# A hybrid decoder layer in split fp32: products with w's high half first, and Strassen pairs for the mixer's in and out projections

## The chip, the core and the metric

One core of a Trainium2 chip runs the whole layer. Its engines work in parallel, each through its own queue in order: TensorE (PE) multiplies, VectorE (DVE) and ScalarE (ACT) do element-wise work and empty the accumulators in PSUM, GpSimd (POOL) does a few small steps and issues accumulating DMAs, SyncE (SP) issues the loads. The metric is the device time of one execution in microseconds.

## The reference, cut to what matters

Sequence 256, width 2048, one layer; all in float32.

```
x = x + 0.5 * swiglu(rmsnorm(x, g1), w_gate1, w_up1, w_down1)      # w_gate, w_up: 2048 x 5632
h = rmsnorm(x, g_mix)
a_q, a_k, a_v, m_q, m_k, m_v, m_o, m_i, m_f = split(h @ w_in)      # 1024 1024 1024 512 512 1024 1024 4 4
y_a = diff_attention(a_q, a_k, a_v)        # 4 heads, two causal softmaxes each, their difference times a_v
q, k = silu(causal_conv4(m_q, m_k))
y_b = rmsnorm(mlstm(q, k, m_v, m_i, m_f)) * sigmoid(m_o)           # 4 heads, decays from the gates i and f
x = x + concat(y_a, y_b) @ w_out                                   # 2048 x 2048
x = x + 0.5 * swiglu(rmsnorm(x, g2), w_gate2, w_up2, w_down2)
out = rmsnorm(x, g_final)
```

## The kernel before

**Split products.** Every weight and every activation is written as a high half (a rounded fp32r copy, made by ACT) and a low half (the remainder, made by DVE): `split`, lines 112 to 114. A product of two tiles is then three matmuls into one accumulator (`mm3`, 139 to 143): x high by w high (141), x high by w low (142), x low by w high (143). The stationary side is 128 x 128 of x transposed, the moving side 512 columns of w.

**Plain units.** `units` (174) multiplies a chunk of 512 columns of w by x: for each unit of two k tiles (256 rows of w) it loads 512 KB of weights (or takes half of a 1 MB load, `load_w`), splits them (`split_w`), and multiplies them by both token halves (`hb` 0 and 1): 2 x 2 x 3 = 12 matmuls. `linear` (213) runs all units of a chunk: 96 matmuls.

**Strassen pairs.** `Paired` (322) takes two chunks at once, wa and wb. The 2 x 2 blocks (two k tiles by two chunks against two token halves by two k tiles) are multiplied in seven products (Strassen's scheme in Winograd's form) rather than eight: a pair costs 21 matmuls, not 24. `first` (337) loads the pair's four tiles, makes three sums on DVE (350, 352), splits sums and tiles, and issues four of the products into four accumulator banks; `combine` (364) adds the banks up with two ACT copies and four DVE operations; `second` (386) issues the other three products (`bare`, `upper`) and, as plain units, the k tiles that are in no pair, for the first chunk; `third` (417) yields the plain units of the second chunk one by one. x needs sums too: `sum_pair` (265). `NP` = 4 of 8 pairs are made so in the feed-forward projections.

**The chain.** `Chain.run` (444) weaves runs together: while the pairs of a new run are issued, the plain units of the last run's second chunk (`third`) are issued between them; then come the new run's `combine`, the end of the old chunk, and the new run's `second`. Small steps that become ready (transposes of a finished part, say) are put on the list `pending`, and `flush` issues all of them at once: behind the first step of `second`, and in `units` before unit 3.

**The mixer.** Only the two feed-forward parts use pairs. The mixer's chunks are all `linear`: three narrow ones for the mLSTM's q and k (392, 384, 256 columns), two for m_v (761 to 770), two each for a_q and a_k (826 to 829), two for a_v (885), two for m_o (903). Between them stand, each as a block over four heads: convolution and SiLU, the mLSTM's score matrices (773 to 788), its numerators (799 to 810), the attention's scores and softmax (833 to 867), and the weighted sums (886 to 899). The out projection (926 to 930) is four `units` streams.

**What sets the order.** The kernel is written as one program; a scheduler places each engine's instructions by priority. `tc.high_priority(offset=AHEAD)` moves loads, splits and a few chains of small steps forward by 400 places, so that they run ahead of the products that use them; how far is limited by the buffers (4 tiles each for wh and wl, 6 accumulator banks, 21 slots for transposed activations). After that each engine runs strictly in its order and waits on semaphores.

## Time and profile before

| | |
|---|---|
| median of 3 runs | 1826.5 us (1823.06 to 1829.19) |
| the profiled execution | 1824.08 us |
| its span, first to last instruction | 1822.4 us |
| mean granted clock of TensorE | 0.998 of 2.4 GHz |
| PE, DVE, ACT, POOL busy | 98%, 82%, 62%, 9% |
| bytes moved | 397.72 MB, 218 GB/s |
| first feed-forward part, mixer and out projection, second feed-forward part | to about 720 us, to about 1130 us, to the end |

A busy share says how long an engine had an instruction in flight; matmuls overlap, so two kernels with PE at 98% may differ in how many matmuls they run per microsecond. "Idle before" and "waits" count the time in which PE had nothing in flight, and name what ended it.

### The profile page before, as it was taken

What the parts mean: (1) busy time and instruction counts of PE and PEld (TensorE: products, weight loads), DVE (VectorE), ACT (ScalarE), POOL (GpSimd) and SP (SyncE); (2) the same over time, 40 slices, a digit from 0 to 9 for tenths busy, and PEclk for the clock granted to TensorE, in tenths of its full rate; (3) what the DMA queues carried; (4) which work ended last, traced back from release to release, by engine and by line L of the source; (5) the groups of instructions that cost most, each with busy time, mean ns of one, the idle gap of its engine ahead of it and who ended that gap; (6) DMA issues with size and microseconds to landing.
All of it is one profiled execution on the core that took longest, in us unless ns stands there. A gap on an engine that the chain in (4) does not pass through costs nothing.

```text
span 1822.4 us, 22684 instructions
## 1 busy us (share of the span) xinstructions
PE 1794.6 (98%) x8090; PEld 1468.2 (81%) x8090; DVE 1488.8 (82%) x1775; ACT 1121.7 (62%) x1443; POOL 156.3 (9%) x199
## 2 busy tenths in 40 slices
PE   8999999999999999999999999999999999999998
PEld 6788788878887888978888888788787888887886
DVE  6889889988998887674465578899889988998886
ACT  6666666666666666554455456666666666666664
POOL 0001100111002100000000000101110021002100
PEclk9999999999999999999999999999999999999999
DMA  8667877797688874553544565677877798678864
GB/s 333 215 204 235 222 234 232 246 250 220 210 252 247 259 237 146 200 185 121 185 159 164 185 213 179 199 228 241 234 230 225 256 247 243 208 230 256 253 190 155
DMA packets 114449, 397.72 MB, mean 218 GB/s; under 512 B 12960, under 2 KB 12960, under 8 KB 107424
## 3 DMA queue, kind: packets, MB, share of 16 engines
q1 hardware_dynamic: 88560, 349.28, 55.5%
q0 software_dynamic: 24480, 44.58, 14.2%
q10 hardware_dynamic: 1296, 2.42, 0.4%
q8 instruction: 63, 1.03, 0.2%
q14 instruction: 50, 0.41, 0.1%
HBM read 349.56 MB, written 2.10 MB: 193 GB/s over the span
## 4 chain that ended last, share of the span: by engine, by line
PE 76%; DMA 9%; DVE 8%; issue 4%; ACT 2%; SPq 1%; POOL 0%; POOLq 0%; DVEq 0%; ACTq 0%
PE acc L142 24%; PE acc L143 24%; PE acc L141 24%; DMA raw<-in_wu_dram 6%; DVE wl L114 5%; ACT wh L113 2%; DVE sums L350 2%; DMA raw<-raw 1%; PE tr L296 1%; SPq L166 1%; DMA xres<-in_x_dram 1%; DVE raw L352 1%; DMA xraw<-in_xt_dram 1%; DMA raw<-in_wd_dram 0%; PE num L808 0%
## 5 line engine op out<-in xcount | busy, mean ns | idle before, releaser
L113 ACT CAST wh<-raw 128x1024 fp32r<-128x1024 f32 (+3 forms) x503 | 464.3, 931 | 377.2 <-PE acc L143 360.9
L114 DVE TENSOR_TENSOR wl<-raw,wh 128x1024 fp32r<-128x1024 f32 (+3 forms) x503 | 535.1, 1074 | 194.7 <-ACT wh L113 191.1
L142 PE MATMUL acc<-wl,xt 128*128 128x512 f32 (+3 forms) x1632 | 630.4, 386 | 4.2 <-DVE wl L114 4.0
L141 PE MATMUL acc<-wh,xt 128*128 128x512 f32 (+3 forms) x1632 | 630.7, 387 | 2.6 <-ACT xt L108 1.5
L143 PE MATMUL acc<-wh,xt 128*128 128x512 f32 (+3 forms) x1632 | 628.8, 386 | 1.2 <-DVE xt L109 1.2
L114 DVE TENSOR_TENSOR wl<-rawp,wh 128x1024 fp32r<-128x1024 f32 x284 | 346.7, 1222 | 43.8 <-ACT wh L113 37.1
L113 ACT CAST wh<-rawp 128x1024 fp32r<-128x1024 f32 x284 | 298.8, 1053 | 117.1 <-PE acc L143 96.4
L141 PE MATMUL acc<-wh,xs 128*128 128x512 f32 x902 | 355.7, 397 | 8.4 <-ACT wh L113 4.0
L142 PEld LDWEIGHTS acc<-wl,xt 128*128 128x128 f32 x1632 | 306.5, 188 | 67.9 <-DVE wl L114 8.8
L141 PEld LDWEIGHTS acc<-wh,xt 128*128 128x128 f32 x1632 | 306.0, 188 | 65.5 <-ACT wh L113 2.8
L143 PEld LDWEIGHTS acc<-wh,xt 128*128 128x128 f32 x1632 | 306.3, 188 | 62.1 <-DVE xt L109 2.5
L142 PE MATMUL acc<-wl,xs 128*128 128x512 f32 x902 | 352.7, 391 | 1.3 <-DVE wl L114 1.1
L143 PE MATMUL acc<-wh,xs 128*128 128x512 f32 x902 | 350.9, 390 | 0.1
L113 ACT CAST wh<-sums 128x1024 fp32r<-128x1024 f32 x122 | 128.4, 1053 | 144.4 <-PE acc L143 139.2
L141 PEld LDWEIGHTS acc<-wh,xs 128*128 128x128 f32 x902 | 169.1, 188 | 57.2 <-ACT u L371 9.3
L142 PEld LDWEIGHTS acc<-wl,xs 128*128 128x128 f32 x902 | 169.4, 188 | 38.9 <-DVE wl L114 6.4
L143 PEld LDWEIGHTS acc<-wh,xs 128*128 128x128 f32 x902 | 169.3, 188 | 36.0 <-DVE xs L109 1.0
L361 POOL DMA_DIRECT2D raw<-raw x122 | 104.0, 853 | 1030.9 <-DVE wl L114 973.7
L350 DVE TENSOR_TENSOR sums<-raw 128x1024 f32<-128x1024 f32 x122 | 149.2, 1223 | 39.4 <-DMA raw<-in_wu_dram 29.2
L114 DVE TENSOR_TENSOR wl<-sums,wh 128x1024 fp32r<-128x1024 f32 x122 | 149.0, 1222 | 14.7 <-ACT wh L113 14.7
L352 DVE TENSOR_TENSOR raw<-sums,raw 128x512 f32<-128x512 f32 x122 | 83.8, 687 | 0.5
L282 POOL DMA_DIRECT2D xres<-part x48 | 43.6, 1060 | 238.2 <-ACT part L281 238.2
(194 smaller groups left out, 756.0 us busy)
## 6 DMA issues: line engine op xcount, KB each, us to landing
rawp<-in_wd_dram SPq DMA_DIRECT2D x96, 512.0 KB, 5.7
rawp<-in_wu_dram SPq DMA_DIRECT2D x94, 512.0 KB, 7.6
raw<-in_wg_dram SPq DMA_DIRECT2D x89, 512.0 KB, 6.7
rawp<-in_wg_dram SPq DMA_DIRECT2D x86, 512.0 KB, 5.7
raw<-in_wu_dram SPq DMA_DIRECT2D x82, 512.0 KB, 7.5
raw<-in_wd_dram SPq DMA_DIRECT2D x80, 512.0 KB, 6.3
raw<-in_win_dram SPq DMA_DIRECT2D x40, 1024.0 KB, 4.8
raw<-raw POOLq DMA_DIRECT2D x122, 256.0 KB, 6.3
```

The lines of the kernel that those rows point to most:

```text
L113: nc.scalar.copy(hi, src)
L114: nc.vector.tensor_tensor(out=lo, in0=src, in1=hi.bitcast(F32), op=ALU.subtract)
L141: nc.tensor.matmul(acc, lh, rh, start=first, stop=False, skip_group_check=on)
L142: nc.tensor.matmul(acc, lh, rl, start=False, stop=False, skip_group_check=on)
L143: nc.tensor.matmul(acc, ll, rh, start=False, stop=last, skip_group_check=on)
L166: nc.sync.dma_start(dst, w[k // LK][:, k % LK:k % LK + 2, :])
L282: nc.gpsimd.dma_start(xres[:, hb, c * CW:(c + 1) * CW], t, accum_op=ALU.add)
L296: nc.tensor.transpose(tr[:, i, hb * P:(hb + 1) * P], hs[hb][:, k * P:(k + 1) * P], ident)
L350: nc.vector.tensor_tensor(out=sums, in0=raw[:, 0:4:3, :], in1=raw[:, 2:3, :].to_broadcast([P, 2, CW]), op=ALU.add)
L352: nc.vector.tensor_tensor(out=raw[:, 2, :], in0=sums[:, 0, :], in1=raw[:, 3, :], op=ALU.add)
L361: nc.gpsimd.dma_start(raw[:, 2, :], raw[:, 1, :], accum_op=ALU.add)
```

## The change

- `mm3` is replaced by `mms`, which takes a list of products: for each, x high by w high and x low by w high (lines 145 and 146 of the changed kernel), and only then, for each, x high by w low (148). A list is one half of a pair's first products (two products), a `bare` or `upper` step, or a whole plain unit with both token halves.
- In the mixer, a_q, m_v, a_k, a_v and m_o (in this order) are five chained `Paired` runs with `NP_MIX` = 3 pairs of eight; the out projection is two, with `NP_OUT` = 2. The third of the narrow q/k chunks is put into the chain as a stream of plain units with loads of their own.
- The blocks over four heads are cut into steps for one head. `side` holds the convolution and gate steps, `mid` the scores, numerators, attention and weighted sums; `aside` issues one of each per step of a run. `flush(n)` issues the first n entries of `pending`. In the run of the first two out-projection chunks, two entries are issued ahead of the first pair (`lead`).
- `vec` and `act` wrap DVE and ACT so that each small operation gets the priority of `soon()` (440 places ahead). The convolution's first step goes from DVE to ACT and its SiLU is done per head and in place. `xp2` and `yT` get sums for their first pairs. The gate matrices use a transpose bank rather than an accumulator bank.

The core of the diff:

```
-    def mm3(acc, lh, ll, rh, rl, first, last, on=False):
-        nc.tensor.matmul(acc, lh, rh, start=first, stop=False, skip_group_check=on)
-        nc.tensor.matmul(acc, lh, rl, start=False, stop=False, skip_group_check=on)
-        nc.tensor.matmul(acc, ll, rh, start=False, stop=last, skip_group_check=on)
+    def mms(jobs):
+        for acc, lh, ll, rh, rl, first, last, on in jobs:
+            nc.tensor.matmul(acc, lh, rh, start=first, stop=False, skip_group_check=on)
+            nc.tensor.matmul(acc, ll, rh, start=False, stop=False, skip_group_check=on)
+        for acc, lh, ll, rh, rl, first, last, on in jobs:
+            nc.tensor.matmul(acc, lh, rl, start=False, stop=last, skip_group_check=on)
...
-                self.prod(self.p5, j, S1, f, 0, at, end)
-                self.prod(self.p7, j, S3, f, 1, at, end)
-                self.prod(self.p1, j, A1, e, 0, at, end)
-                self.prod(self.p6, j, S2, e, 1, at, end)
+                mms([self.job(self.p5, j, S1, f, 0, at, end), self.job(self.p7, j, S3, f, 1, at, end)])
+                mms([self.job(self.p1, j, A1, e, 0, at, end), self.job(self.p6, j, S2, e, 1, at, end)])
...
+    def flush(n=None):
+        now = pending[:n]
+        del pending[:n]
+        for f in now:
             f()
...
+    class Early:
+        def __init__(self, engine):
+            self.engine = engine
+        def __getattr__(self, op):
+            def run(*args, **kwargs):
+                with soon():
+                    return getattr(self.engine, op)(*args, **kwargs)
+            return run
+    vec, act = Early(nc.vector), Early(nc.scalar)
+    side, mid = [], []
+    def aside(work):
+        if work:
+            work.pop(0)()
...
             for i in range(max(self.ns, len(self.rest))):
+                aside(side)
...
-                if i == 0:
+                if i % 2 == 0:
                     flush()
+                aside(mid)
...
+        def run(self, p, half, end, last_units=1, lead=()):
             done = 0
+            for f in lead:
+                next(self.stream)
+                done += 1
+                f()
             for i, _ in enumerate(p.first()):
                 while done < (i + 1) * self.steps // p.ns:
                     next(self.stream)
                     done += 1
+                flush(1)
+                aside(side)
...
+    def conv(acc, src, h, i):
+        w = lambda j: prm[:, G_CW + j * 8 + i:G_CW + j * 8 + i + 1]
+        a = acc[:, h, :]
+        act.activation(a, src[:, h, :], AF.Identity, scale=w(3), bias=prm[:, G_CB + i:G_CB + i + 1])
+        for d in (1, 2, 3):
+            vec.scalar_tensor_tensor(a[:, d:], src[:, h, :S - d], w(3 - d), a[:, d:], op0=ALU.mult, op1=ALU.add)
+        act.activation(a, a, AF.Silu)
...
+    def both(c):
+        return Paired(xp2, win[c], win[c + 1], KD, NP_MIX)
...
+    chain.run(both(2), to_T(qT), to_T(qT))
+    by_head(scores)
+    chain.run(both(0), functools.partial(take_mv, 0), functools.partial(take_mv, 1))
+    by_head(numerators)
+    chain.run(both(4), to_T(kT), to_T(kT))
+    by_head(attend)
+    chain.run(both(6), take_av, take_av)
+    chain.run(both(8), functools.partial(gate_out, 0), functools.partial(gate_out, 1))
...
-    for c in range(4):
-        accs = []
-        chain.put(units(accs, yT, wout[c], KD, fine=c == 3), KD // UK, functools.partial(finish_out, c, accs))
-        if c < 3:
-            chain.finish()
+    for c in (0, 2):
+        chain.run(Paired(yT, wout[c], wout[c + 1], KD, NP_OUT), functools.partial(finish_out, c),
+                  functools.partial(finish_out, c + 1),
+                  lead=() if c else [functools.partial(flush, 1)] * 2)
```

Two places show what this does to PE's order. The first is a pair's first products in the first feed-forward part; `wh` and `wl` are the weights' halves, `xs` the token sums' halves, and the `acc` tiles four accumulator banks. PE's rows before:

```order
L141 MATMUL acc_417_2067<-wh_419_2071,xs_4_133 128x512 [waits Activation_49]
L142 MATMUL acc_417_2067<-wl_420_2072,xs_4_133 128x512 [waits DVE_49]
L143 MATMUL acc_417_2067<-wh_419_2071,xs_5_134 128x512
L141 MATMUL acc_416_2066<-wh_419_2071,xs_4_133 128x512
L142 MATMUL acc_416_2066<-wl_420_2072,xs_4_133 128x512
L143 MATMUL acc_416_2066<-wh_419_2071,xs_5_134 128x512
L141 MATMUL acc_414_2064<-wh_422_2076,xs_4_133 128x512 [waits Activation_49]
L142 MATMUL acc_414_2064<-wl_423_2077,xs_4_133 128x512 [waits DVE_49]
L143 MATMUL acc_414_2064<-wh_422_2076,xs_5_134 128x512
L141 MATMUL acc_415_2065<-wh_422_2076,xs_4_133 128x512 [waits Activation_49]
L142 MATMUL acc_415_2065<-wl_423_2077,xs_4_133 128x512
L143 MATMUL acc_415_2065<-wh_422_2076,xs_5_134 128x512
```

Each accumulator's three products stand together. In the changed kernel:

```order
L145 MATMUL acc_417_2067<-wh_419_2071,xs_4_133 128x512 [waits Activation_49]
L146 MATMUL acc_417_2067<-wh_419_2071,xs_5_134 128x512
L145 MATMUL acc_416_2066<-wh_419_2071,xs_4_133 128x512
L146 MATMUL acc_416_2066<-wh_419_2071,xs_5_134 128x512
L148 MATMUL acc_417_2067<-wl_420_2072,xs_4_133 128x512 [waits DVE_49]
L148 MATMUL acc_416_2066<-wl_420_2072,xs_4_133 128x512
L145 MATMUL acc_414_2064<-wh_422_2076,xs_4_133 128x512 [waits Activation_49]
L146 MATMUL acc_414_2064<-wh_422_2076,xs_5_134 128x512
L145 MATMUL acc_415_2065<-wh_422_2076,xs_4_133 128x512 [waits Activation_49]
L146 MATMUL acc_415_2065<-wh_422_2076,xs_5_134 128x512
L148 MATMUL acc_414_2064<-wl_423_2077,xs_4_133 128x512 [waits DVE_49]
L148 MATMUL acc_415_2065<-wl_423_2077,xs_4_133 128x512
```

The products with `wl` stood second in each product and now stand behind all four with `wh`; the number of matmuls is the same.

The second is the mLSTM's numerators in the mixer: `num` is an accumulator bank, `mv` the values, `dec` a head's weighted scores. PE's rows before:

```order
L808 MATMUL num_1433_7090<-mv_1393_6878,dec_1420_7040 128x257 [waits PE_49,Activation_49,Pool_49]
L808 MATMUL num_1434_7094<-mv_1393_6878,dec_1420_7040 128x257 [waits DVE_49]
L808 MATMUL num_1434_7094<-mv_1394_6881,dec_1420_7040 128x257 [waits Pool_49]
L808 MATMUL num_1435_7099<-mv_1393_6878,dec_1423_7053 128x257 [waits PE_49,Activation_49]
L808 MATMUL num_1436_7103<-mv_1393_6878,dec_1423_7053 128x257 [waits DVE_49]
L808 MATMUL num_1436_7103<-mv_1394_6881,dec_1423_7053 128x257
L808 MATMUL num_1437_7108<-mv_1417_7029,dec_1426_7066 128x257 [waits PE_49,Activation_49,Pool_49]
L808 MATMUL num_1438_7112<-mv_1417_7029,dec_1426_7066 128x257 [waits DVE_49]
L808 MATMUL num_1438_7112<-mv_1418_7032,dec_1426_7066 128x257 [waits Pool_49]
L808 MATMUL num_1439_7117<-mv_1417_7029,dec_1429_7079 128x257 [waits DVE_49,PE_49]
L808 MATMUL num_1440_7121<-mv_1417_7029,dec_1429_7079 128x257 [waits DVE_49,PE_49]
L808 MATMUL num_1440_7121<-mv_1418_7032,dec_1429_7079 128x257
```

All twelve stand in one row. In the changed kernel, the step of the second head and the products behind it:

```order
L846 MATMUL num_1578_7705<-mv_1518_7430,dec_1489_7274 128x257 [waits DVE_49,PE_49]
L846 MATMUL num_1579_7709<-mv_1518_7430,dec_1489_7274 128x257 [waits DVE_49,PE_49]
L846 MATMUL num_1579_7709<-mv_1519_7433,dec_1489_7274 128x257
L145 MATMUL acc_1520_7436<-wh_1580_7714,xs_1261_6022 128x512 [waits Activation_49]
L146 MATMUL acc_1520_7436<-wh_1580_7714,xs_1262_6023 128x512
L145 MATMUL acc_1522_7438<-wh_1580_7714,xs_1261_6022 128x512
L146 MATMUL acc_1522_7438<-wh_1580_7714,xs_1262_6023 128x512
L148 MATMUL acc_1520_7436<-wl_1581_7715,xs_1261_6022 128x512
L148 MATMUL acc_1522_7438<-wl_1581_7715,xs_1261_6022 128x512
L145 MATMUL acc_1523_7439<-wh_1582_7724,xs_1261_6022 128x512 [waits Activation_49]
```

The numerators of all four heads stood in one row; now each head's three stand alone between products of the run's second half. Between one head's step and the next stand 24, 21 and 12 products, and the same numbers between the heads' scores and between the heads' attention steps.

## Rows read from the trace of the kernel before

**Rows 1.** The page, parts 1 and 4: busy engines, the chain by line.

```profile
PE 1794.6 (98%) x8090; PEld 1468.2 (81%) x8090; DVE 1488.8 (82%) x1775; ACT 1121.7 (62%) x1443; POOL 156.3 (9%) x199
...
PE acc L142 24%; PE acc L143 24%; PE acc L141 24%; DMA raw<-in_wu_dram 6%; DVE wl L114 5%; ACT wh L113 2%; DVE sums L350 2%; DMA raw<-raw 1%; PE tr L296 1%; SPq L166 1%; DMA xres<-in_x_dram 1%; DVE raw L352 1%; DMA xraw<-in_xt_dram 1%; DMA raw<-in_wd_dram 0%; PE num L808 0%
```

**Rows 2.** Timeline of PE: start us, length us, line, operation, tiles, count.

```profile
1050.07 0.39 PE L142 MATMUL acc<-wl,xt 128*128 128x512 f32 x1
...
1052.11 0.39 PE L142 MATMUL acc<-wl,xt 128*128 128x512 f32 x1
```

**Rows 3.** Windows: length, busy us (x count) by engine, clock, DMA, GB/s.

```profile
100.00:700.00 600.00, 595.70 (x2641) 486.01 (x2640) 534.92 (x586) 383.79 (x455) 66.09 (x82) 1.00 0.79 236
700.00:1140.00 440.00, 439.72 (x2121) 369.91 (x2120) 272.54 (x413) 238.65 (x372) 8.90 (x12) 1.00 0.49 171
1140.00:1700.00 560.00, 554.12 (x2453) 451.44 (x2452) 507.49 (x559) 362.00 (x427) 66.47 (x77) 1.00 0.78 233
```

**Rows 4.** What PE waited for: us in total, times, longest us.

```profile
PE acc L142 <- DVE wl L114: 5.1, 12, 0.8
PE acc L141 <- ACT wh L113: 4.9, 9, 0.7
...
PE acc L141 <- ACT u L371: 1.3, 2, 0.9
```

**Rows 5.** Groups on DVE by shape: xcount | busy us, mean ns | idle.

```profile
L114 DVE TENSOR_TENSOR wl<-raw,wh 128x1024 fp32r<-128x1024 f32 x355 | 434.1, 1223 | 172.1 <-ACT wh L113 169.2
...
L350 DVE TENSOR_TENSOR sums<-raw 128x1024 f32<-128x1024 f32 x122 | 149.2, 1223 | 39.4 <-DMA raw<-in_wu_dram 29.2 <-DMA raw<-in_wd_dram 5.5 <-DVE wl L114 2.7
...
L114 DVE TENSOR_TENSOR wl<-raw,wh 128x512 fp32r<-128x512 f32 x132 | 86.2, 686 | 11.0 <-ACT wh L113 10.4
L352 DVE TENSOR_TENSOR raw<-sums,raw 128x512 f32<-128x512 f32 x122 | 83.8, 687 | 0.5
...
L370 DVE TENSOR_TENSOR acc<-acc,u 128x512 f32<-128x512 f32 x37 | 25.6, 693 | 0.0
```

**Rows 6.** The page, parts 5 and 6: a split on ACT, the accumulating DMA.

```profile
L113 ACT CAST wh<-rawp 128x1024 fp32r<-128x1024 f32 x284 | 298.8, 1053 | 117.1 <-PE acc L143 96.4
...
raw<-raw POOLq DMA_DIRECT2D x122, 256.0 KB, 6.3
```

**Rows 7.** Timeline of PE, a wait for wl; in brackets idle before.

```profile
206.74 0.39 PE L141 MATMUL acc<-wh,xt 128*128 128x512 f32 x1
207.64 0.50 PE L142 MATMUL acc<-wl,xt 128*128 128x512 f32 x1 [0.51 <-DVE wl L114]
207.97 0.40 PE L143 MATMUL acc<-wh,xt 128*128 128x512 f32 x1
```

**Rows 8.** Timeline of PE at the start of the second feed-forward part.

```profile
1141.99 0.73 PE L143 MATMUL acc<-wh,xt 128*128 128x512 f32 x2 [1.05 <-DVE xt L109]
```

**Rows 9.** Windows around scores and numerators (first three) and attention (last).

```profile
813.70:821.80 8.10, 8.10 (x40) 5.14 (x39) 2.98 (x5) 4.24 (x12) 0.00 (x0) 1.00 0.55 209
821.80:825.20 3.40, 3.40 (x11) 2.75 (x10) 1.05 (x3) 0.81 (x3) 0.00 (x0) 0.50 0.00 0
825.20:829.00 3.80, 3.80 (x20) 3.34 (x18) 2.77 (x12) 0.00 (x0) 0.00 (x0) 1.00 0.00 0
919.00:927.00 8.00, 8.00 (x59) 6.78 (x58) 6.38 (x21) 6.83 (x24) 0.00 (x0) 1.00 0.49 188
```

**Rows 10.** Groups of attention's softmax, 915 to 945 us, by shape.

```profile
L849 ACT ACTIVATE aexp<-sc,amx 128x256 f32<-128x256 f32 x8 | 3.7, 475 | 0.8 <-DVE amx L847 0.6
...
L849 ACT ACTIVATION_READ_ACCUMULATOR aexp<-sc,amx 128x1 f32 x16 | 3.3, 209 | 0.0
...
L849 ACT ACTIVATE aexp<-sc,amx 128x128 f32<-128x128 f32 x8 | 2.9, 379 | 1.8 <-DVE amx L847 1.8
...
L846 DVE TENSOR_REDUCE amx<-sc 128x2 f32<-128x256 f32 x4 | 1.7, 420 | 1.2 <-PE sc L844 1.2
...
L847 DVE TENSOR_SCALAR amx<-amx 128x2 f32<-128x2 f32 x8 | 1.3, 164 | 0.0
```

More of the change, by code (lines that the diff above doesn't have):

```diff
@@ L179, in units, with products @@
         accs += [ps_acc.tile([P, CW], F32, tag="acc", name=nm("acc"))[:, 0:n] for _ in range(NT)]
-        def products(hb, u, rh, rl):
-            for t in range(UK):
-                k = u * UK + t
-                mm3(accs[hb], *halves(xp, k, hb), rh[:, t, :], rl[:, t, :], k == 0, k == nk - 1)
+        def products(hbs, u, rh, rl):
+            ks = [(t, u * UK + t) for t in range(UK)]
+            mms([(accs[hb], *halves(xp, k, hb), rh[:, t, :], rl[:, t, :], k == 0, k == nk - 1, False)
+                 for hb in hbs for t, k in ks])
         nu = nk // UK
@@ L209, in units @@
         for t in tail:
[L210 removed]
+            products((1,), *t)
         yield
@@ L373, in combine, with plain, products @@
                 nc.vector.tensor_tensor(out=p5, in0=p5, in1=u2, op=ALU.subtract)
-        def plain(self, w, k, accs, hbs=(0, 1)):
+        def plain(self, w, k, accs, apart=False):
             rh, rl = split_w(load_unit(w, self.k0 + k), (UK,))
-            def products(hb):
-                for t in range(UK):
-                    mm3(accs[hb], *halves(self.xp, k + t, hb), rh[:, t, :], rl[:, t, :],
-                        False, k + t == self.rest[-1] + UK - 1, True)
-            products(0)
-            return functools.partial(products, 1)
+            def products(hbs):
+                mms([(accs[hb], *halves(self.xp, k + t, hb), rh[:, t, :], rl[:, t, :],
+                      False, k + t == self.rest[-1] + UK - 1, True) for hb in hbs for t in range(UK)])
+            products((0,) if apart else (0, 1))
+            return functools.partial(products, (1,))
         def second(self):
@@ L411, in second @@
                 if i < len(self.rest):
-                    self.plain(self.wa, self.rest[i], (n11, n21))()
-                if i == 0:
+                    if i < len(self.rest) - 1:
+                        self.plain(self.wa, self.rest[i], (n11, n21))
+                    else:
+                        self.plain(self.wa, self.rest[i], (n11, n21), True)()
+                if i % 2 == 0:
                     flush()
+                aside(mid)
             return [n11, n21]
@@ L420, in third @@
             for i, k in enumerate(self.rest):
-                other = self.plain(self.wb, k, (self.p5, self.p6))
-                if i < len(self.rest) - last_units:
-                    other()
-                else:
+                apart = i >= len(self.rest) - last_units
+                other = self.plain(self.wb, k, (self.p5, self.p6), apart)
+                if apart:
                     tail.append(other)
@@ L656, in run @@
                     nc.tensor.transpose(tr[:, hb * P:(hb + 1) * P], t[:, hb, j * P:(j + 1) * P], ident)
-                nc.scalar.copy(mT[i // NH][:, i % NH, :], tr)
+                act.copy(mT[i // NH][:, i % NH, :], tr)
         pending.append(run)
-        done += nct
-    flush()
+    for c in range(2):
+        finish_qk(c, linear(xp2, wqk[c], KD))
+    accs = []
+    chain.put(units(accs, xp2, wqk[2], KD, fine=True), KD // UK, functools.partial(finish_qk, 2, accs))
     def ct(shape, name):
@@ L878, in y_transposes, with weighted @@
                                     ident)
+        if kt // 2 < NP_OUT:
+            sum_pair(yT, kt // 2, gained(tr, g))
+            return
+        hi, lo = plain_pair(yT, kt // 2)
         for i in range(2):
-            g = gain[:, (kt + i) % 8:(kt + i) % 8 + 1]
-            nc.scalar.activation(hi[:, i, :], tr[:, i, :], AF.Copy, scale=g)
-            nc.vector.scalar_tensor_tensor(lo[:, i, :], tr[:, i, :], g, hi[:, i, :].bitcast(F32),
+            act.activation(hi[:, i, :], tr[:, i, :], AF.Copy, scale=g[:, i:i + 1])
+            vec.scalar_tensor_tensor(lo[:, i, :], tr[:, i, :], g[:, i:i + 1], hi[:, i, :].bitcast(F32),
                                            op0=ALU.mult, op1=ALU.subtract)
-    av = proj_tok(6)
-    for h in range(NH):
+    later = []
+    def weighted(h):
         ps = ps_acc.tile([P, NT, VD], F32, tag="acc", name=nm("av"))
-        vs = [v[:, h * VD:(h + 1) * VD] for v in av]
+        vs = [av[h // 2][:, hb, h % 2 * VD:(h % 2 + 1) * VD] for hb in range(NT)]
         nc.tensor.matmul(ps[:, 0, :], wts[h][:, 0:P], vs[0], start=True, stop=True)
```

248 lines of the change are left out of this document (118 added, 130 removed).

## The prediction

> **What bounds the kernel now.** I began with the page's first part and its chain of waits [rows 1]: TensorE (PE) has a matmul in flight for 1794.6 of 1822.4 us, VectorE (DVE) is busy for 82%, and the chain that ended last lies to 72% in the three product lines 141 to 143, 24% each. A busy share of overlapping matmuls doesn't tell how close PE is to its pace, so I went to the timeline: in an undisturbed stretch nine products of 512 columns start within 2.04 us, 227 ns apart [rows 2]. The kernel has 7,314 such products (2,534 calls of `mm3` with three each, less the 288 narrower ones of the q/k projection); 7,314 x 0.227 is 1660 us, and the rest is narrow products, transposes, head, tail and waits. So each product taken out is worth 227 ns wherever PE isn't waiting for something else. The windows by stage [rows 3] say where it might: both feed-forward parts run DVE at 89 to 91% with PE at 99%, the mixer and the out projection (700 to 1140 us) run DVE at 62% with PE at 99.9%. PE is the limit everywhere, and the mixer has room on DVE that the feed-forward parts lack. Last, the list of what PE waited for [rows 4]: 5.1 us for a low half of the weights (wl, from DVE) in 12 waits, 4.9 for a high half (wh, from ScalarE, ACT), and 1.3 for the copy that opens a Strassen combine.
>
> **Fewer products.** A Strassen pair takes 7 x 3 = 21 products where two plain units on two chunks take 8 x 3 = 24. The five in-projection runs have three such pairs each, the two out-projection runs two each: 19 pairs x 3 = 57 products less, 7,257 stay, and the order of the changed kernel shows that many. 57 x 0.227 = **12.9 us off**, all of it on the path as long as PE stays the limit in the mixer.
>
> **What pays for them on DVE and ACT.** A plain unit costs DVE one subtraction of 1024 columns, 1.22 us; two units on two chunks, which a pair replaces, 2.44. A pair costs the sums (1.22), the third sum (0.69), three subtractions of 1024 (3.67) and one of 512 (0.69): 6.27, so 3.8 more [rows 5]. 19 pairs: 73 us. Seven combines more, four operations of 0.69 each: 19 us. Six more token pairs with their sums, some 1.5 us each from the 0.69 us subtraction and three small ones: 9 us. One convolution step of four goes to ACT: -3. Together +98 us. DVE then has 272.5 + 98 = 370 us of work in about 430 us, 86%, which is less than the 89% at which the feed-forward part keeps PE at 99% [rows 3]. So I cost this DVE work at nothing; its cover is PE's own products, and if that cover were gone, the excess over PE's time would show one to one. The loads move the same bytes in 512 KB pieces; in the mixer the DMA engines stand at 0.49 against 0.79 in the feed-forward part, so that is free too. The pairs' accumulating DMAs (19 more on POOL's queue) land 6.3 us after their issue [rows 6] and are needed in the run's second half, some 50 products or 11 us later; POOL is busy for 9 of the mixer's 440 us.
>
> **The order within a unit.** Before, the product with wl is the second one of the unit, 0.23 us after the first; now it stands behind all products with wh: fifth in a Strassen half (0.91 us after the start), ninth in a plain unit (1.8 us). The trace shows what one late wl costs [rows 7]: the first product starts at 206.74, the second at 207.64 instead of 206.97 (0.67 us lost, of which the row counts 0.51 as idle), and the one after it another 0.10 late. Lost are 0.77 us where the row says 0.51, a factor of 1.5. 5.1 us x 1.5 = 7.7 us for the 12 waits. The longest is 0.8 us idle, so nearly every one fits into the new delay of 0.68 or 1.6 us. What is late next is the next unit's wh, which ACT makes one step ahead of the same wl. I take **6.5 us off**. Bounds: 7.7 if all goes, 0 if each wait only moves to the next wh. The same edit asks for x's low half one or two products earlier (0.23 to 0.45 us), which counts where that half is just ready, as at 1141 us, where PE sat idle 1.05 us [rows 8]; that goes into the small waits below.
>
> **The numerators' slow stretch.** Before, the four heads' score matmuls (from 813.7 us on) and then 24 numerator matmuls stand in a row. The granted clock is 1.00 to 821.8 us, 0.50 from there to 825.2, and 1.00 again [rows 9]: 3.4 us at the lower level of 1.2 GHz. 11 matmuls run in them; at the pace of the stretch behind (20 in 3.8 us, 0.19 each) it would have been 18. Seven times 0.19 are 1.3 us. The change puts 12 to 24 wide products between one head and the next, so I expect PE to stay at 2.4 GHz: **1.3 us off** (bounds 0 and 1.7, half of the slow stretch).
>
> **New small waits.** In the changed kernel scores, numerators, attention and weighted sums of a head are issued into the two accumulator banks that a run leaves free, so a head's first matmul waits, at the front of PE's in-order queue, until ACT and DVE have emptied the banks of the head before, and the whole second half stands behind it. Scores, numerators and attention have three such re-uses each, nine in all, and the weighted sums use one bank a head, three more: twelve. Between the heads stand 24, 21 and 12 products: 5.4, 4.8 and 2.7 us. The longest emptying is attention's [rows 10]: reduce 0.42, scale 0.16, two exponentials of 128 columns with their accumulator reads, 2 x 0.59, two of 256 with theirs, 2 x 0.68: 3.1 us. That fits twice and misses 2.7 us by 0.4 us, by up to 1.7 us when a 1.22 us split sits in front on DVE. The other kinds are shorter. The trace of before has no such spacing, so the bounds are: none (0), or a DVE split's 1.22 us at each of the twelve, 15 us. I take 1.5 us for attention's last head, 1 us for the out projection's entry (its first two token pairs are transposed one unit ahead of their use, and the chain of sums behind a transposition is longer than that unit's 2.7 us), and 1 us for the x halves and for the combine, whose first copy can now start only one product before the pair's end rather than three (PE waits for that copy twice today, 1.3 us [rows 4]): **3.5 us on**, near the lower bound, because the lengths in the row are near the products' lengths.
>
> **Sum.** -12.9 - 6.5 - 1.3 + 3.5 = -17.2 us. The profiled execution took 1824.08 us (span 1822.4), 2.4 below the median of 1826.5; the sum is made against it and gives 1806.9, and against the median **1809.3**. I predict 1809.
>
> **Rivals.**
> - *The wl waits come back as wh waits.* ACT copies wh in the same order in which DVE subtracts, so a late unit may stay late. For it: 4.9 us of waits for wh already [rows 4]. Against it: the waits end on DVE, and ACT is at 64% in the feed-forward part. Then the 6.5 us are lost: 1816.
> - *More goes than counted.* All of 7.7 us, no new wait: 12.9 + 7.7 + 1.3 = 21.9, 1804.6; with the scatter of the runs (3.4 below the median) 1801.
> - *The two free banks bind, slower.* Each of the twelve re-uses finds ACT's and DVE's queues filled with splits at both hops: 3.1 + 2 x (1.22 on DVE + 1.05 on ACT [rows 6]) = 7.6 us of emptying against 4.3 us of products on average, 3.3 us lost twelve times, 40 us. Without my 3.5: -20.7 + 40 gives 1846. It makes the kernel slower from 1.7 us a re-use on. Against it: in the changed order these operations stand ahead of the splits in both queues, and DVE has 14% free.
> - *The clock falls at every head, slower.* In the trace of the mixer it fell once, after 8.1 us without a wide product [rows 9]. If twelve head re-uses and four last ones each cost the 1.7 us of such a stretch: 27 us instead of a gain of 1.3; -12.9 - 6.5 + 3.5 + 27 gives 1838. Against it: before the fall the small matmuls of four heads stood together, now those of one (a quarter of it, 2 us), and the attention of before, 8 us almost all of small matmuls from 919 us on, kept 1.00 [rows 9]. The Trainium skill ("TensorE: Matmul & The Clock Gate", section "A second HAM failure mode: psum-queue depth-cycling") speaks for this rival: a kernel that cycled PSUM banks and idled briefly between groups of matmuls kept falling back to the low clock. By that rule the change, which interleaves groups and waits for banks, would be a loss; the one fall in this trace came at the longest such row of groups and not at the shorter ones, so it agrees only in part.
>
> That the pairs would not be there is excluded by the order (57 products fewer).
>
> **Chances.** The forecast 0.60 (1803 to 1815), the first rival 0.20, more than counted 0.11, the banks 0.06, the clock 0.03. A measurement of this kernel can tell some 0.3%, 5.5 us, from no change. Faster by more than that (under 1821): 0.86; within it: 0.09, the tails of the forecast and of the first rival, and a milder form of the banks; slower: 0.05. The range of 8 in 10 goes from 1801 (the second rival with the scatter) to 1820, which holds the first rival and a sum with 0 for the order and 7.5 us of new waits (12.9 + 1.3 - 7.5 = 6.7).
>
> **What would show it.** Right: the pace stays 227 ns; the wait of line 148's products for wl falls from 5.1 us to under 1; the mixer, from the end of the first feed-forward part to the second's first gate products, is about 10 us shorter with PE at 99% and DVE near 86%; the granted clock stays at 1.00 there; the feed-forward windows lose 3 us each. Wrong: PE's waits for wh grow by what the waits for wl lose (first rival); waits of a microsecond and more in front of the score, numerator and attention matmuls (banks); granted clock of 0.50 near them (clock); or DVE over 95% in the mixer with PE waiting for the sums, which would mean that I undercounted its work.

## The result and the profile after

The changed kernel takes **1807.7 us** (median; 1805.68 to 1809.69) against 1826.6 for the kernel before: ratio 0.9895, 95% interval 0.9877 to 0.9913, 19 us faster. Forecast were 1809 and the range 1801 to 1820. The profiled execution's span fell from 1822.4 to 1803.9 us.

The page of the changed kernel, parts 1 and 4 (as [rows 1]):

```profile
PE 1777.9 (99%) x8033; PEld 1461.1 (81%) x8033; DVE 1571.9 (87%) x1889; ACT 1170.5 (65%) x1523; POOL 174.1 (10%) x218
...
PE acc L145 27%; PE acc L146 27%; PE acc L148 27%; DMA raw<-raw 3%; DVE wl L116 2%; PE tr L301 1%; ACT wh L115 0%; DMA raw<-in_wd_dram 0%; POOL xres L287 0%; PE sc L895 0%; POOL raw L385 0%; PE tr L248 0%; PE num L846 0%; DVE sums L376 0%; 
```

PE runs 57 matmuls fewer (8090 to 8033) and the three product lines now carry 81% of the chain, not 72%. The windows of the changed kernel, moved a little to fit its stages (as [rows 3]):

```profile
100.00:690.00 590.00, 585.75 (x2606) 481.17 (x2605) 527.08 (x576) 379.50 (x447) 65.83 (x77) 1.00 0.79 237
700.00:1116.00 416.00, 415.87 (x2009) 348.85 (x2009) 348.40 (x514) 278.11 (x438) 26.66 (x35) 1.00 0.61 187
1150.00:1680.00 530.00, 526.35 (x2344) 432.68 (x2343) 483.47 (x533) 344.99 (x406) 61.60 (x72) 1.00 0.79 235
```

What PE waited for in the changed kernel (as [rows 4]):

```profile
PE acc L145 <- ACT u L395: 5.8, 7, 1.1
PE acc L145 <- ACT wh L115: 2.4, 3, 1.3
PE acc L145 <- ACT sg L314: 2.2, 5, 1.3
PE tr L248 <- ACT xg L333: 1.7, 2, 1.0
PE acc L148 <- DVE wl L116: 1.4, 3, 0.9
...
PE acc L145 <- ACT u L392: 0.8, 3, 0.3
```

The wait for wl fell from 5.1 us to 1.4 and the one for wh from 4.9 to 2.4. What rose is the wait for the combine's two copies (u), from 1.3 to 6.6; that for xg, in front of transposes, is new.

**Where the time went.** I cut both traces at the same products: the start of the 2,901st product of 512 columns (near the end of the first feed-forward part), the first product of 392 columns (the q/k projection), and the 2,500th product of 512 columns counted from the last (inside the second feed-forward part). The last two cuts in the timeline of before:

```profile
719.45 0.34 PE L141 MATMUL acc<-wh,xt 128*128 128x392 f32 x1
...
1229.83 0.39 PE L143 MATMUL acc<-wh,xs 128*128 128x512 f32 x1
```

And in that of the changed kernel:

```profile
716.84 0.34 PE L145 MATMUL acc<-wh,xs 128*128 128x392 f32 x1
...
1213.36 0.39 PE L145 MATMUL acc<-wh,xs 128*128 128x512 f32 x1
```

With the spans these give four stages (us; the last three columns are experiments of the next section):

| stage | before | changed | order alone | old order | both edits, three sums |
|---|---|---|---|---|---|
| A: to the 2,901st product | 696.1 | 691.0 | 691.3 | 694.7 | 690.4 |
| B: the mixer's entry | 23.4 | 25.9 | 23.2 | 27.4 | 22.3 |
| C: mixer, out projection, entry of the second part | 510.4 | 496.5 | 509.6 | 497.7 | 495.1 |
| D: rest | 592.5 | 590.6 | 590.7 | 592.9 | 590.5 |

These are single executions, one of each kernel; two of the changed kernel differ by up to 1.5 us in a stage (below). The change took 5.1 us off in A, 13.9 in C and 2.0 in D, and added 2.5 in B. The added time stands in one place of the changed kernel's timeline of PE:

```profile
693.93 1.03 PE L248 MATMUL tr<-ident,xres 128*128 128x128 f32 x8
696.00 0.66 PE L248 MATMUL tr<-ident,xres 128*128 128x128 f32 x4 [1.03 <-ACT xg L333]
697.34 0.66 PE L248 MATMUL tr<-ident,xres 128*128 128x128 f32 x4 [0.68 <-ACT xg L333]
698.33 0.50 PE L145 MATMUL acc<-wh,xs 128*128 128x512 f32 x1 [0.34 <-ACT u L392]
```

Four tiles of transposes come in a row; there are two transpose banks, so the third and the fourth tile wait until ACT has emptied a bank (xg). 2.05 us idle.

### The profile page after: what moved, and what is told of

Same layout as the page of the kernel before. It is cut to its first block, busy times and chain, and to the rows that moved or that the text cites. A ratio compares the mean times of both kernels' runs of the same rounds, so it can differ in the third digit from the quotient of the medians.

```text
span 1803.9 us, 23316 instructions
## 1 busy us (share of the span) xinstructions
PE 1777.9 (99%) x8033; PEld 1461.1 (81%) x8033; DVE 1571.9 (87%) x1889; ACT 1170.5 (65%) x1523; POOL 174.1 (10%) x218
## 3 DMA queue, kind: packets, MB, share of 16 engines
q0 software_dynamic: 27216, 49.56, 16.2%
q8 instruction: 63, 1.03, 0.2%
## 4 chain that ended last, share of the span: by engine, by line
PE 85%; DMA 4%; DVE 3%; issue 2%; ACT 1%; POOL 1%; SPq 0%; POOLq 0%; DVEq 0%; ACTq 0%
PE acc L145 27%; PE acc L146 27%; PE acc L148 27%; DMA raw<-raw 3%; DVE wl L116 2%; PE tr L301 1%; ACT wh L115 0%; DMA raw<-in_wd_dram 0%; POOL xres L287 0%; PE sc L895 0%; POOL raw L385 0%; PE tr L248 0%; PE num L846 0%; DVE sums L376 0%; DVE acc L394 0%
## 5 line engine op out<-in xcount | busy, mean ns | idle before, releaser
L115 ACT CAST wh<-raw 128x1024 fp32r<-128x1024 f32 (+3 forms) x448 | 400.8, 907 | 245.1 <-PE acc L146 202.4
L145 PE MATMUL acc<-wh,xt 128*128 128x512 f32 (+2 forms) x1392 | 539.5, 389 | 1.4 <-ACT wh L115 0.8
L146 PE MATMUL acc<-wh,xt 128*128 128x512 f32 (+2 forms) x1392 | 538.4, 388 | 0.8 <-DVE xt L111 0.8
L116 DVE TENSOR_TENSOR wl<-raw,wh 128x1024 fp32r<-128x1024 f32 (+3 forms) x448 | 460.3, 1040 | 56.2 <-ACT wh L115 50.4
L116 DVE TENSOR_TENSOR wl<-rawp,wh 128x1024 fp32r<-128x1024 f32 (+1 forms) x358 | 431.7, 1209 | 69.3 <-ACT wh L115 57.6
L115 ACT CAST wh<-rawp 128x1024 fp32r<-128x1024 f32 (+1 forms) x358 | 372.7, 1043 | 154.4 <-PE acc L146 133.3
L145 PE MATMUL acc<-wh,xs 128*128 128x512 f32 (+2 forms) x1123 | 441.5, 396 | 10.3 <-ACT u L395 5.8
L146 PE MATMUL acc<-wh,xs 128*128 128x512 f32 (+2 forms) x1123 | 434.4, 389 | 0.5 <-DVE xs L111 0.5
L148 PE MATMUL acc<-wl,xt 128*128 128x512 f32 (+2 forms) x1392 | 388.1, 388 | 1.4 <-DVE wl L116 1.4
L148 PE MATMUL acc<-wl,xs 128*128 128x512 f32 (+2 forms) x1123 | 347.6, 387 | 0.1
L145 PEld LDWEIGHTS acc<-wh,xt 128*128 128x128 f32 x1392 | 261.2, 188 | 55.5 <-ACT xt L110 1.4
L146 PEld LDWEIGHTS acc<-wh,xt 128*128 128x128 f32 x1392 | 261.5, 188 | 54.1 <-DVE xt L111 1.6
L145 PEld LDWEIGHTS acc<-wh,xs 128*128 128x128 f32 x1123 | 211.4, 188 | 62.8 <-ACT u L395 11.0
L146 PEld LDWEIGHTS acc<-wh,xs 128*128 128x128 f32 x1123 | 211.6, 189 | 41.5 <-DVE xs L111 1.7
```

The source lines that it names most:

```text
L115: nc.scalar.copy(hi, src)
L116: nc.vector.tensor_tensor(out=lo, in0=src, in1=hi.bitcast(F32), op=ALU.subtract)
L145: nc.tensor.matmul(acc, lh, rh, start=first, stop=False, skip_group_check=on)
L146: nc.tensor.matmul(acc, ll, rh, start=False, stop=False, skip_group_check=on)
L148: nc.tensor.matmul(acc, lh, rl, start=False, stop=last, skip_group_check=on)
```

## The experiments

All ratios are to the kernel before, run beside each.

### The order alone, and the old order in the changed kernel

The first is the kernel before with `mms`, and no pairs in the mixer:

```
-    def mm3(acc, lh, ll, rh, rl, first, last, on=False):
+    def mms(jobs):
...
```

> The kernel before with one edit: within each unit all products with w's high half come first. No pair is added in the mixer. Theory (the order alone is worth about 6.5 to 7 us, since it takes waits for a low half of w off TensorE, and the 57 fewer products are a separate gain): about 1819.5 us, 7 us under the kernel before run beside it, in the two feed-forward parts, with the wait for wl falling from 5.1 us to about 1.4 and the waits for the combine's copies rising. Rival (the order only moves each wait to the next high half or to the combine, and the whole gain comes from the mixer): within 2 us of the kernel before.

The second is the changed kernel with the order within a unit as before:

```
-            nc.tensor.matmul(acc, ll, rh, ...)
-        for acc, lh, ll, rh, rl, first, last, on in jobs:
-            nc.tensor.matmul(acc, lh, rl, ..., stop=last, ...)
+            nc.tensor.matmul(acc, lh, rl, ...)
+            nc.tensor.matmul(acc, ll, rh, ..., stop=last, ...)
```

> The changed kernel with the order within a unit put back as it was (x high by w high, x high by w low, x low by w high); the pairs and the small steps stay. Theory (the two parts add up): about 6.5 to 7 us slower than the changed kernel, 1814.5 us, with the waits for wl back at about 5 us in the feed-forward parts. Rival 1 (the order gives nothing): 1808. Rival 2 (the mixer with pairs, whose VectorE is at 84%, needs the order more than the mixer before did): more than 9 us slower, 1817 or over, with waits for wl inside the mixer.

The order alone: 1817.5 us, 7.4 under the median of before; ratio 0.9965 (0.9952 to 0.9979). The old order: 1814.5, 6.8 over the changed kernel's 1807.7, which was measured beside other runs; ratio 0.9939 (0.9927 to 0.9951). By the ratios the order alone takes 6.4 us off and all the rest of the change alone 11.1, together 17.5; the changed kernel, measured twice (0.9895 above, 0.9911 below), is 19.2 and 16.2 faster. So the two halves add up within the noise. PE's waits with the order alone (L146 is there the product with wl):

```profile
PE acc L143 <- ACT u L372: 5.4, 6, 1.1
PE acc L146 <- DVE wl L114: 2.4, 4, 1.3
...
PE acc L143 <- ACT wh L113: 1.4, 4, 0.4
```

And in the changed kernel with the old order:

```profile
PE acc L146 <- DVE wl L116: 6.1, 11, 1.4
PE acc L145 <- ACT wh L115: 6.0, 9, 1.4
...
PE acc L145 <- ACT u L394: 0.5, 1, 0.5
```

With either kernel around it, the new order takes waits for wl and wh away and brings the wait for the combine's second copy. The list of waits holds only a part of the gain. PE's busy time with the order alone (the page, part 1):

```profile
PE 1788.3 (99%) x8090; PEld 1470.5 (81%) x8090; DVE 1486.5 (82%) x1775; ACT 1126.9 (62%) x1443; POOL 156.6 (9%) x199
```

That is 6.3 us less than before for the same 8090 matmuls, while the idle time (span less busy time) fell only from 27.8 to 26.6 us. 1.3 of the 6.3 are the slow stretch that this execution lacks (see the account of the prediction). The rest goes with products that start late while the one before is still in flight, which counts as busy: in A and D, starts later than 227 ns after the last without idle time add up to 13.2 us before and 10.3 with the order alone.

### Fewer and more pairs

Two constants of the changed kernel, 1 and 1 in the first run, 4 and 3 in the second:

```
-NP_MIX = 3
-NP_OUT = 2
+NP_MIX = 1
+NP_OUT = 1
```

> The changed kernel with one pair a run in the mixer and one in the out projection rather than three and two: 12 pairs fewer, so 36 products more. Theory (TensorE's pace sets the mixer's time and VectorE's work there costs nothing): 36 x 0.227 = 8.2 us slower than the changed kernel, 1816. Rival (VectorE sets the mixer's time, and 46 us less of its work gives some of it back): under 4 us slower.

> The changed kernel with four pairs a run in the mixer and three in the out projection rather than three and two: 7 pairs more, so 21 products fewer, and about 27 us more on VectorE, which then stands near 90% in the mixer. Theory (TensorE still sets the time): 4.8 us faster than the changed kernel, 1803. Rival (the mixer's small steps leave VectorE no more room, and its queue is late for sums and low halves): no gain or a loss, with waits of TensorE for the sums (xs, xt) and for wl in the mixer.

Fewer pairs: 1819.8 us, 12.1 over the changed kernel (ratio 0.9966, 0.9954 to 0.9978), where 8.2 were due. Stage C is 10.5 longer, and 2.3 of it more than the products; the row of transposes, which in the changed kernel stood at the mixer's entry only, has come up in the out projection too, where x is transposed for the second feed-forward part (timeline of PE):

```profile
1064.81 1.03 PE L248 MATMUL tr<-ident,xres 128*128 128x128 f32 x8
1066.82 0.66 PE L248 MATMUL tr<-ident,xres 128*128 128x128 f32 x4 [0.97 <-ACT xg L333]
1068.16 0.66 PE L248 MATMUL tr<-ident,xres 128*128 128x128 f32 x4 [0.69 <-ACT xg L333]
```

More pairs, four and three: 1814.0, **6.3 slower** than the changed kernel (ratio 0.9937, 0.9925 to 0.9949, clear of both measurements of the changed kernel) where 4.8 faster were due; stage C 2.4 longer, D 4.0. My theory of this run fell; the runs with four pairs and with three out-projection pairs below take it apart.

### The heads together

`mid`, emptied in one step rather than one head per step:

```
-                aside(mid)
+                while mid:
+                    aside(mid)
```

> The changed kernel, with the four heads' scores (and likewise their numerators, attention and weighted sums) issued in one row rather than one head per step with 12 to 24 wide products between. Theory (the spacing is what keeps the head's bank waits and the low clock away): a head's matmuls then wait at the front of TensorE's queue until the banks of the head before are emptied; for attention three times 3.1 us of emptying less about 1 us of its own matmuls, 6 us, about 1 us each for the other three kinds, and 1.3 us of a stretch at the lower clock: about 10 us slower than the changed kernel, 1818, with waits in front of the score, attention and numerator matmuls. Rival (VectorE and ScalarE empty the banks fast enough in either order): within 2 us.

1809.5 us against 1807.5 for the changed kernel run beside it: ratios 0.9917 (0.9903 to 0.993) and 0.9911 (0.9898 to 0.9925), not to be told apart. The wait that is new stands in front of the weighted sums (timeline of PE):

```profile
980.41 0.70 PE L951 MATMUL av<-pt,awT 128*128 128x256 f32 x2 [0.53 <-DVE ya L333]
...
982.18 0.70 PE L951 MATMUL av<-pt,awT 128*128 128x256 f32 x2 [0.20 <-DVE ya L333]
```

Scores, numerators and attention had none, and the granted clock fell nowhere between 7 and 1803 us. PE's order kept a few wide products between the heads' numerators even so. The spacing of a head is worth 2.0 us by the medians, less than the scatter, and not 10.

### The end of a pair, and the place of the pending step

In the last pair of a run, the banks that the combine reads first (p1, which it copies, and p6) are filled first:

```
-                mms([self.job(self.p5, j, S1, f, 0, at, end), self.job(self.p7, j, S3, f, 1, at, end)])
-                mms([self.job(self.p1, j, A1, e, 0, at, end), self.job(self.p6, j, S2, e, 1, at, end)])
+                fs = [self.job(self.p5, j, S1, f, 0, at, end), self.job(self.p7, j, S3, f, 1, at, end)]
+                es = [self.job(self.p1, j, A1, e, 0, at, end), self.job(self.p6, j, S2, e, 1, at, end)]
+                for js in (es, fs) if end else (fs, es):
+                    mms(js)
```

> The changed kernel, with the four products of the last pair of a run in another order: the two that the combine copies first (p1, p6) ahead of the other two (p5, p7). Theory (the 5.8 us in which TensorE waits for the combine's second copy stand there because in the new order the accumulators are finished only at the end of the pair): the copies start 1.4 us earlier and most of these waits go, 4 to 5 us faster than the changed kernel, 1803. Rival (ScalarE or VectorE, late for another reason such as an accumulating DMA, sets the copies' start): no change within 2 us, and the waits stay.

And, in `Chain.run`, `flush(1)` ahead of the old run's units:

```
             for i, _ in enumerate(p.first()):
+                flush(1)
                 while done < (i + 1) * self.steps // p.ns:
                     next(self.stream)
                     done += 1
-                flush(1)
```

> The changed kernel, with the one pending step that a pair issues (transposes, for example) placed ahead of the old run's plain units rather than behind them. Theory (the mixer's entry loses 2.5 us because four tiles of transposes come in a row over two banks with no products between): a tile then has products behind it, the 2.5 us mostly go, 1805. Rival (the transposes wait for x itself, which is not ready earlier): no change, or a new wait of the same size in front of the transposes.

> The changed kernel unchanged, as the reference beside the three others and as a second profile of it. The variants with fewer or more pairs had waits at the part boundaries of the second feed-forward part that were 2.6 and 4.4 us longer than here, though every engine has the same order of instructions there. Theory (these waits scatter from execution to execution): this second profile differs from the first one there by 1 to 4 us. Rival (they belong to the program, by where its buffers and transfers stand): the second profile has the same waits at the same places within 0.3 us, and the median is 1807.7 again.

The first: 1802.6 us, ratio 0.9884 (0.987 to 0.9898). PE's waits, to be read beside the changed kernel's list above (L397 is the second copy there):

```profile
PE acc L145 <- ACT wh L115: 4.1, 8, 1.1
PE acc L145 <- ACT u L397: 2.1, 3, 1.0
...
PE acc L145 <- ACT u L394: 0.3, 1, 0.3
```

The waits for the copies fell from 6.6 to 2.4 us (6.0 in the second profile of the changed kernel), and part of that came back as waits for wh, 4.1 against 2.4 and 3.2. Stage D shows the gain best: 587.9 us, against 590.6 and 591.2, and no wait for a copy is left in it. Why the copies were late is seen at one part boundary of the changed kernel. ACT, DVE and PE there:

```profile
182.37 0.58 ACT L392 COPY u<-acc 128x512 f32<-128x512 f32 x1
...
185.09 0.59 ACT L395 COPY u<-acc 128x512 f32<-128x512 f32 x1 [1.10 <-DVE acc L394]
...
182.50 1.23 DVE L116 TENSOR_TENSOR wl<-raw,wh 128x1024 fp32r<-128x1024 f32 x1 [1.68 <-ACT wh L115]
183.64 0.68 DVE L393 TENSOR_TENSOR u<-acc,u 128x512 f32<-128x512 f32 x1
184.36 0.70 DVE L394 TENSOR_TENSOR acc<-acc,u 128x512 f32<-128x512 f32 x1
...
184.27 0.40 PE L145 MATMUL acc<-wh,xt 128*128 128x512 f32 x1
185.73 0.51 PE L145 MATMUL acc<-wh,xs 128*128 128x512 f32 x1 [1.06 <-ACT u L395]
```

The chain copy, add, add, copy is 0.58 + 0.68 + 0.70 + 0.59 = 2.55 us of work; it took 3.3 from 182.37, because the first add stood behind a 1.23 us subtraction, and PE ran out of the old run's products 1.06 us before its end.

The second: 1801.9 us, ratio 0.9881 (0.9863 to 0.9899). Stage B is 22.3 us, 3.6 less than in the changed kernel, and no wait is left in it: each tile of transposes now has the old run's products behind it. The median is 5.6 us under the changed kernel's, where 2.5 were due; the profiled executions differ by 3.5, B's part, and the four runs spread from 1799.8 to 1807.4, so what is over B's 3.6 is not shown.

The changed kernel again: 1807.5 us, ratio 0.9911. Its second profile differs from the first by -1.1, +1.5, +0.8 and +0.7 us in the four stages. So a stage scatters by up to 1.5 us between two executions of one kernel; the 1.5 in B is a fall of the clock (last section). In D the two differ by less than the 1 to 4 us of the theory. The 4.0 us of stage D in the run with four and three pairs are more than that, but every engine's order of instructions is the same there as in the changed kernel, and the four kernels of the next part, which share one order in D, spread from 589.3 to 594.4. In one of them, three pairs in the out projection (593.3), D holds a wait of 2.0 us for wl at 1246.6 us and a fall of the clock behind it. What else sets D within these 5 us stays open.

### Both edits, and the number of pairs once more

> The changed kernel with both edits that made it faster alone: p1 and p6 first in the last pair of a run (4.9 us) and the pending step ahead of the old run's plain units (5.6 us). Theory (they take away different waits, the combine's copies at part boundaries and the transposes at the mixer's entry): the gains add up, 1797 to 1798. Rival (both only move the same wait to the high halves of w): 1801 to 1802, as with either alone.

> As the kernel with both edits, but with four pairs a run in the mixer rather than three: 5 pairs more, 15 products fewer. In the variant with four and three pairs, waits stood at the combine of one mixer run (1.4 us) and at the out projection's entry (2 us and more). Theory (TensorE's pace sets the mixer, and what made that variant slower were three pairs in the out projection): 15 x 0.227 = 3.4 us faster than the kernel with both edits. Rival (VectorE at 89% in the mixer is late for the combine and low halves there): 0 to 3 us slower, with waits for u and wl between 840 and 960 us.

> As the kernel with both edits, but with three pairs a run in the out projection rather than two: 2 pairs more, 6 products fewer, and one token pair more that has to be transposed and summed ahead of its first use. Theory (the out projection's entry is what made the variant with four and three pairs slower): the transposes there wait for two banks, 2 us and more, so 1 to 4 us slower in spite of 1.4 us of products. Rival (TensorE's pace decides there too): 1.4 us faster.

Both edits: 1801.5 us, ratio 0.9866 (0.9852 to 0.9881). By the medians that is no more than either alone, by the ratio 2.7 us more, and the intervals overlap: whether the gains add up isn't settled by the medians. In the stages B keeps its 22.3 and C is 495.2, but in A (694.7) this execution had a wait of 1.8 us at 564 us with a clock of 0.50 for 3.4 us behind it, and a wait of 1.1 at 626.

Four pairs in the mixer: 1805.8 us, 4.3 slower by the medians than the kernel with both edits (ratio 0.9884, 0.9867 to 0.9901) where 3.4 faster were due. The two intervals overlap a little; that it isn't 3.4 faster (a ratio of 0.9847) is clear. Stage C is 499.3 against 495.2: 4.1 longer in spite of 15 products fewer, 7.5 in all. Two places show it. In the numerators (DVE, then PE, of the kernel with four pairs):

```profile
893.37 1.23 DVE L376 TENSOR_TENSOR sums<-raw 128x1024 f32<-128x1024 f32 x1
894.52 0.42 DVE L333 COPY hm<-num 128x256 f32<-128x256 f32 x1
894.85 0.15 DVE L333 COPY den<-num 128x1 f32<-128x1 f32 x1
894.92 1.21 DVE L116 TENSOR_TENSOR wl<-sums,wh 128x1024 fp32r<-128x1024 f32 x1
896.05 0.42 DVE L333 COPY hm<-num 128x256 f32<-128x256 f32 x1
...
895.14 0.47 PE L145 MATMUL acc<-wh,xs 128*128 128x512 f32 x1 [0.28 <-DVE den L333]
896.68 0.47 PE L145 MATMUL acc<-wh,xs 128*128 128x512 f32 x1 [0.84 <-DVE den L333]
```

The next run's first products need the two free banks that the last head's numerators still hold; the copies that empty them stand behind a sum and a subtraction of 1.2 us each. This is the forecast's rival of the two free banks, at one head and not at twelve places. The other place is the out projection's entry (timeline of PE):

```profile
1000.08 0.66 PE L936 MATMUL tr<-ident,ya 128*128 128x128 f32 x4 [0.53 <-ACT xg L333]
1001.47 0.66 PE L936 MATMUL tr<-ident,ya 128*128 128x128 f32 x4 [0.73 <-ACT xg L333]
1003.16 1.23 PE L145 MATMUL acc<-wh,xs 128*128 128x512 f32 x3 [1.03 <-ACT xs L115]
```

In the kernel with both edits only two of these tiles follow on each other, and 15 products of the new run stand ahead of the next one (1000.39 to 1004.13 us there); with four pairs three stand in a row. Why they were placed so isn't shown. The granted clock fell to 0.50 for 3.4 us from 1003.7 on. Idle at the two places is 1.1 + 2.3 us, the clock up to 1.7 more: about 5 of the 7.5. DVE was busy for 101.6 of the 120 us from 840 to 960, 85%, so it is not out of time; it is late at single points.

Three pairs in the out projection: 1801.7 us, ratio 0.9869 (0.9854 to 0.9884), the same as with two; stage C 0.1 longer where the products give 1.4 less. One wait of 0.95 us at its entry takes most of that. The 1 to 4 us of my theory were too much.

The last run takes the mixer's unused sums away:

```
-        pending.append(functools.partial(chunk_to_xt, c, G_MIX, xp2, NP))
+        pending.append(functools.partial(chunk_to_xt, c, G_MIX, xp2, NP_MIX))
```

> As the kernel with both edits, but the mixer's x gets token sums for three pairs rather than four (the fourth pair's sums are made and never used). That takes four small subtractions and two copies off VectorE and ScalarE at the end of the first feed-forward part. Theory (VectorE's work there costs nothing as long as TensorE has products behind the transposes): the same within 2 us, 1800 to 1803. Rival (the chain of sums at the mixer's entry holds up the low halves behind it): 2 to 4 us faster, 1798.

1800.0 us, ratio 0.9856 (0.9836 to 0.9875): within the theory, and not to be told from the kernel with both edits. Its median is the lowest here, 7.6 us under the changed kernel's.

## Why the prediction was right, point by point

**Fewer products: right.** 12.9 us forecast; stage C gave 13.9, of which 13.1 with the order the same (order alone against changed) and 12.7 with the old order. With one pair a run C lost 10.5 us: the 8.2 of the 36 products, and 2.0 idle at a row of transposes.

**DVE's work at nothing: right at three pairs, wrong as a rule.** DVE stood at 348.4 of 416 us, 84% (86% forecast; its busy time rose by 83.1 us over the whole kernel, where 98 were counted), and PE waited for nothing between 720 and 1127 us. With four pairs the mixer lost time at 87% (361.5 of 416 us). The forecast took the 89% of the feed-forward part as proof of room; there no small step of a head needs DVE at a given moment.

**The order: right in size, only half by its reason.** 6.5 us forecast, 7.4 and 6.8 measured by the two runs. That a late wl costs more than its idle time, which the factor of 1.5 stood for, is borne out: with the order alone most of the gain is busy time. The wl waits fell as forecast, to 1.4 rather than under 1. But what is late next was put down as wh, and those waits halved; it was the combine's copies. The step that failed is the 1 us for "the x halves and the combine": the copies alone rose by 5.3 us of idle time. With them repaired, wh waits do rise again (4.1 to 6.1 us in the five profiles with that edit, 2.4 and 3.2 in the changed kernel), so the first rival describes what comes after. That the sum held in spite of this was luck: the forecast names nothing that would make up for it. Of stage A's 5.1 us, 3.0 stand in its first 400 products; the order alone has 2.6 of them and the kernel with the old order 2.6 too, and none of the other profiles passes the 400th product as late as that one of before. So this part can't be put down to the order; its cause is open.

**The slow stretch: not shown.** The changed kernel has no low clock in the mixer, as forecast. But the kernel with the order alone issues the four heads in a row as before, and its clock did not fall either. Its windows (clock third from the right):

```profile
813.00:821.00 8.00, 8.00 (x41) 6.16 (x40) 3.74 (x12) 2.44 (x9) 0.00 (x0) 1.00 0.25 100
821.00:829.00 8.00, 8.00 (x37) 6.69 (x36) 3.41 (x13) 4.89 (x13) 0.00 (x0) 1.00 0.00 0
```

The 24 numerators (timeline of PE, before and then the order alone):

```profile
822.62 6.66 PE L808 MATMUL num<-mv,dec 128*128 128x257 f32 x24
...
817.45 5.37 PE L809 MATMUL num<-mv,dec 128*128 128x257 f32 x24
```

The 1.29 us between them bear out the forecast's price of a fall. But [rows 9] showed what one execution did, not what the row of heads costs, and the 1.3 us are not a gain that the change can claim.

**New small waits: 3.5 us, in wrong places and too little.** Attention's last head (1.5) and the out projection's entry (1) cost nothing in the changed kernel; the mixer's entry, which the forecast doesn't name, cost 2.5, and the combine's copies 5.3 and not 1. The copies' part is inside the 7.4 and 6.8 us of the order, so the terms as measured are 13.1 (products with the order the same), some 7 (order), 0 (slow stretch) and 2.5 on: 17.6 off, where 17.2 were forecast. The forecast counted the transposes' chain of sums at the out projection and overlooked that the same `flush` issues x's.

**The rivals.** Slower by the banks: in the changed kernel no such wait at all; with four pairs it appeared, at one place. Slower by the clock: in the changed kernel the heads never lowered it. The Trainium skill ("TensorE: Matmul & The Clock Gate", section "A second HAM failure mode: psum-queue depth-cycling") reports a clock that kept falling back in a kernel that cycled banks and idled briefly between groups of matmuls; the rows of transposes told of below agree in part, three falls in seven profiles; the heads did not wait, and show neither.

## What to carry to other kernels

A product order that gives a late operand more time also moves the end of the other accumulators: look at what is released by each accumulator's last product, and fill those first that others copy first. Small steps fit between products as long as something stands behind each of them; count the banks a row of transposes or heads needs, and put products behind every tile that has to wait for one. Spare busy time of an engine is no measure of room where single steps are due at a given product: try one step more on the chip before counting on it.

## What the runs showed of the hardware

The granted clock fell for 3.4 us, not only at the end, in some executions and not in others with the same instructions. In the second profile of the changed kernel (windows; clock third from the right):

```profile
697.10:700.50 3.40, 3.23 (x8) 2.55 (x9) 3.40 (x7) 2.16 (x6) 0.00 (x0) 0.50 0.02 5
...
1140.80:1144.20 3.40, 3.40 (x9) 2.65 (x9) 1.23 (x1) 1.23 (x2) 0.90 (x1) 0.50 0.68 230
```

Both begin behind idle time of PE, at the row of transposes and at the second feed-forward part's entry (1.31 us there). The first profile has the same 1.03 and 0.68 us of idle time at 696 us and a clock of 1.00 behind it:

```profile
698.30:701.70 3.40, 3.37 (x15) 2.78 (x16) 3.40 (x7) 2.16 (x5) 0.00 (x0) 1.00 0.02 5
```

Seven profiles have this row at the mixer's entry, with 2.05 us of idle time. In three of them the fall follows, and stage B takes 27.35 to 27.43 us; in the other four it takes 25.86 to 25.89. So a wait of 2 us cost 1.5 more in some executions and not in others, and a single profile can't say whether a kernel avoids it. In the thirteen profiles other than that of before, PE had 57 idle times of 1.0 us or more between 100 and 1780 us; the clock fell, to 0.50 for 3.4 us, behind eight of them and nowhere else in that stretch. The fall before, at 821.8 us, has no idle time of PE ahead of it. What decides it is open.
